# Moving the steps of seven-product groups, a weight buffer and a vector load in a two-layer fp32 decoder kernel

## The chip, the cores and the metric

The kernel runs on one core of one Trainium2 chip. A core has a matrix engine (TensorE, PE in the profile; its weight loads are PEld), a vector engine (VectorE, DVE), a scalar engine (ScalarE, ACT), a general engine (GpSimd, POOL) and a queue engine (SyncE, SP). Each works through its own instructions in order and waits for the others by semaphores; transfers between HBM and the on-chip buffers are issued here by SP and POOL. The metric is the device time of one execution in microseconds (us), the median of several runs.

## The reference

A decoder trunk of two layers over 256 tokens of width 2048, in float32. Each layer normalises its input, projects it once, sends it through three token mixers (sparse attention, a convolution module, stick-breaking attention), gates each, and merges the three by sigmoid gates before one output projection:

```python
def hybrid_layer(x, ...):
    h = rms_norm(x, norm_w)
    proj = h @ w_in
    (qa, ka, va, za, qi, ki, wi, ub, zb, qc, kc, vc, zc, gates) = jnp.split(proj, split_points(), axis=-1)
    ...
    y_a = (dsa_attention(qa, ka, va, qi, ki, wi, top_k) * jax.nn.silu(za)) @ w_a_out
    y_b = (conformer_conv(ub, conv_w, conv_b, cln_w, cln_b) * jax.nn.silu(zb)) @ w_b_out
    y_c = (stick_breaking_attention(qc, kc, vc) * jax.nn.silu(zc)) @ w_c_out
    g = jax.nn.sigmoid(gates).reshape(b, s, N_BRANCH, D_MODEL)
    merged = g[:, :, 0] * y_a + g[:, :, 1] * y_b + g[:, :, 2] * y_c
    return x + merged @ w_out

def reference(x, ...):
    for i in range(DEPTH):
        x = hybrid_layer(x, ...)
    return rms_norm(x, final_norm_w)
```

## The kernel before

**Products.** Every float32 operand is split into a high and a low part, and a product is three matmuls: high by high, low by high, high by low. The activations are split once. The weights come in units of 512 KB (128 partitions, 2 blocks of 512 columns): SP loads a unit (L413), ACT casts its high part `wh` (L247, `high`), DVE subtracts to get the low part `wl` (L251, `low`), and PE multiplies (L262). Such a unit is one step: twelve matmuls of 512 columns.

**Homes of the units.** `raw_unit` gives a unit one of five buffers called `raw` (RAWS = 5). Every sixth unit of a stage goes to the tile `va` instead, which is also the tile that holds the values of the stick-breaking attention (`va_pair`, read by PE at L1292). So there are six homes, and a load waits until its home has been read.

**Groups of seven products.** A 2 x 2 block product is done with seven half products (class `Seven`, M1 to M7; each has a half a and a half b, six matmuls each) instead of eight. Some of its weights are sums of blocks, which DVE makes: `two` loads a block into half of the tile `ar` (L469), `three` loads one into `ph` or `pl` (L478), `first_sums` adds them and the unit of M1 (L482, L483), `second_sum` (L487) and, in the output stage, `last_sum` (L491) go on in `ar`. M5, M6, M7 and M4 take their weights from these sums. Partial results are carried between the PSUM banks of a group by ACT (`copied`, L528) and DVE (`fork`, L534). The tiles `ph` and `pl` serve the stick-breaking attention too.

**Order.** A stage is a list of steps, and `run` goes through it: it loads seven steps ahead (PARTS + LOADS), converts two steps ahead (PARTS), and fires events that are tied to a step, the sums and copies among them. `gather` builds such a list from a string: `g.M1a` is half a of product M1 of the group, `y`, `c`, `d`, `e`, `f` each take the next plain step of a list of that name, `c*2` takes two. A scheduler turns the program into one instruction order for each engine; an instruction whose tile is free earlier can stand earlier in its queue than its line suggests.

**The merge and output stage of a layer** (the end of the layer's code, L1519 to L1570) runs as one list: the gates, the projection of the first and the third branch, then `zb`, sixteen plain steps that compute the gate of the second branch, and behind it the group `g1`, which computes merge gates, filled up with steps `y` that project the third branch's last columns; the group `h1`, the second branch's projection `y1`; and then the output projection. In the last layer the output has a group `o` for two of its four column chunks (`e`, `f` finish these) and plain steps for the two others: `c` (chunk 2) and `d` (chunk 3).

What the output multiplies are the merged values. A merged quarter (512 columns) is finished by DVE (L1386, L1387), transposed by DVE (L291), sent through HBM by POOL (`z`, L294) and brought back by POOL (`zy`, L300), and then split by ACT (L620) and DVE (L621) into a tile `s`; `use_m` does the last. Of a plain chunk's eight steps the first four (0 to 3) read the first two quarters, 4 and 5 the third, 6 and 7 the last. The weights of the last norm come in one 1 MB load (L1535).

## Time and profile before

| what | value |
|---|---|
| median of 3 runs (lowest, highest) | 2013.15 us (2013.05, 2013.35) |
| the profiled execution, its own time | 2015.98 us |
| its span (first to last instruction) | 2014.1 us |
| ACT, DVE busy | 1142.7 us (57%), 1715.3 us (85%) |
| mean granted clock of PE | 0.997 |
| HBM, over the span | 228 GB/s |

The table says of each engine how long it was busy in one profiled execution. A row of the timeline gives the start, the duration, the engine, the line of the code, the operation and the tiles (out<-in), and in brackets how long the engine had been idle and what it had waited for. SPq and POOLq are transfers as their engines issue them.

### The profile page before, as it was taken

What the parts mean: (1) busy time and instruction counts of PE and PEld (TensorE: products, weight loads), DVE (VectorE), ACT (ScalarE), POOL (GpSimd) and SP (SyncE); (2) the same over time, 40 slices, a digit from 0 to 9 for tenths busy, and PEclk for the clock granted to TensorE, in tenths of its full rate; (3) what the DMA queues carried; (4) which work ended last, traced back from release to release, by engine and by line L of the source; (5) the groups of instructions that cost most, each with busy time, mean ns of one, the idle gap of its engine ahead of it and who ended that gap; (6) DMA issues with size and microseconds to landing.
All of it is one profiled execution on the core that took longest, in us unless ns stands there. A gap on an engine that the chain in (4) does not pass through costs nothing.

```text
span 2014.1 us, 25976 instructions
## 1 busy us (share of the span) xinstructions
PE 1991.2 (99%) x9266; PEld 1667.6 (83%) x9266; DVE 1715.3 (85%) x2267; ACT 1142.7 (57%) x1327; POOL 171.2 (9%) x284
## 2 busy tenths in 40 slices
PE   9999999999999999999999999999999999999988
PEld 8889888888878888887888988888888788888876
DVE  8667899878989979978885779988879899798776
ACT  7555555565655556555554555455666555565544
POOL 0111112100100000011200111121001000000100
PEclk9999999999999999999999999999999999999999
DMA  7798679855767676787877886788657666767873
GB/s 272 233 285 264 187 220 294 246 178 178 212 204 245 185 221 222 236 259 250 305 229 233 282 242 191 236 275 245 178 178 218 212 218 197 244 210 237 283 239 126
DMA packets 234498, 461.70 MB, mean 229 GB/s; under 512 B 17216, under 2 KB 30016, under 8 KB 234240
## 3 DMA queue, kind: packets, MB, share of 16 engines
q1 hardware_dynamic: 214208, 399.74, 63.5%
q0 software_dynamic: 18496, 57.17, 9.2%
q10 hardware_dynamic: 1664, 3.15, 0.4%
q8 instruction: 72, 1.18, 0.2%
q14 instruction: 58, 0.48, 0.1%
HBM read 427.21 MB, written 32.77 MB: 228 GB/s over the span
## 4 chain that ended last, share of the span: by engine, by line
PE 94%; DMA 2%; DVE 2%; issue 1%; ACT 0%; POOL 0%; DVEq 0%; SPq 0%; POOLq 0%; ACTq 0%
PE acc L262 74%; PE mm L262 17%; DMA ar<-in_w_out_dram 1%; DVE wl L251 1%; DMA va<-in_w_a_dram 1%; PE mm L1099 1%; PE mm L1189 0%; DMA zy<-z 0%; DVE ar L483 0%; PE mm L1292 0%; PE mm L1157 0%; PE mm L1239 0%; ACT wh L247 0%; DMA z<-zt 0%; PE mm L866 0%
## 5 line engine op out<-in xcount | busy, mean ns | idle before, releaser
L262 PE MATMUL acc<-wh,s 128*128 128x512 f32 (+1 forms) x4528 | 1133.9, 390 | 2.5 <-ACT wh L247 2.5
L247 ACT CAST wh<-raw 128x1024 fp32r<-128x1024 f32 (+1 forms) x651 | 680.9, 1048 | 632.1 <-PE acc L262 451.8
L262 PEld LDWEIGHTS acc<-wh,s 128*128 128x128 f32 x4528 | 843.7, 188 | 169.6 <-ACT wh L247 4.5
L251 DVE TENSOR_TENSOR wl<-raw,wh 128x1024 fp32r<-128x1024 f32 (+1 forms) x652 | 789.9, 1215 | 197.4 <-ACT wh L247 195.8
L262 PE MATMUL acc<-wl,s 128*128 128x512 f32 (+1 forms) x2072 | 563.5, 389 | 3.3 <-DVE wl L251 3.1
L262 PEld LDWEIGHTS acc<-wl,s 128*128 128x128 f32 x2072 | 388.1, 188 | 83.8 <-DVE wl L251 6.0
L262 PE MATMUL mm<-wh,s 128*128 128x512 f32 x992 | 248.6, 392 | 6.7 <-ACT s L620 4.2
L294 POOL DMA_DIRECT2D z<-zt x192 | 112.1, 590 | 1404.4 <-DVE zt L291 1388.6
L262 PEld LDWEIGHTS mm<-wh,s 128*128 128x128 f32 x992 | 187.0, 189 | 47.0 <-ACT s L620 4.7
L684 DVE SCALAR_TENSOR_TENSOR s<-yT,cst,s 128x256 f32<-128x256 f32 x480 | 212.1, 479 | 0.0
L262 PE MATMUL mm<-wl,s 128*128 128x512 f32 x496 | 133.6, 392 | 0.5 <-DVE wl L251 0.5
L262 PEld LDWEIGHTS mm<-wl,s 128*128 128x128 f32 x496 | 93.6, 189 | 20.5 <-DVE wl L251 0.9
L247 ACT CAST wh<-ar 128x1024 fp32r<-128x1024 f32 x60 | 63.2, 1053 | 56.5 <-PE acc L262 21.7
L247 ACT CAST wh<-va 128x1024 fp32r<-128x1024 f32 x51 | 53.5, 1049 | 49.5 <-PE acc L262 19.7
L251 DVE TENSOR_TENSOR wl<-va,wh 128x1024 fp32r<-128x1024 f32 x51 | 62.1, 1219 | 20.4 <-ACT wh L247 20.4
L251 DVE TENSOR_TENSOR wl<-ar,wh 128x1024 fp32r<-128x1024 f32 x60 | 73.1, 1219 | 3.2 <-ACT wh L247 2.9
L262 PEld LDWEIGHTS mm<-s,wl 128*128 128x128 f32 x512 | 67.0, 191 | 5.0
L262 PE MATMUL mm<-s,wl 128*128 128x192 f32 x512 | 66.1, 271 | 0.0
L300 POOL DMA_DIRECT2D zy<-z x50 | 35.9, 719 | 298.3 <-DMA z<-zt 104.5
L291 DVE STREAM_TRANSPOSE zt<-acc 128x512 f32<-128x512 f32 (+1 forms) x68 | 45.4, 681 | 3.6 <-PE acc L262 3.0
L620 ACT CAST s<-zy 128x1024 fp32r<-128x1024 f32 x20 | 20.9, 1046 | 13.6 <-DVE zy L670 9.8
L621 DVE TENSOR_TENSOR s<-zy,s 128x1024 fp32r<-128x1024 f32 x20 | 24.4, 1221 | 3.7 <-ACT s L620 3.7
(272 smaller groups left out, 1245.7 us busy)
## 6 DMA issues: line engine op xcount, KB each, us to landing
raw<-in_w_in_dram SPq DMA_DIRECT2D x505, 512.0 KB, 4.5
raw<-in_w_out_dram SPq DMA_DIRECT2D x51, 512.0 KB, 5.4
zy<-z POOLq DMA_DIRECT2D x48, 512.0 KB, 5.8
z<-zt POOLq DMA_DIRECT2D x184, 128.0 KB, 4.4
va<-in_w_in_dram SPq DMA_DIRECT2D x30, 512.0 KB, 3.9
raw<-in_w_a_dram SPq DMA_DIRECT2D x28, 512.0 KB, 4.4
raw<-in_w_c_dram SPq DMA_DIRECT2D x28, 512.0 KB, 4.6
raw<-in_w_b_dram SPq DMA_DIRECT2D x28, 512.0 KB, 4.8
```

What stands on the lines that cost most here:

```text
L247: newest_parts[0] = nc.scalar.copy(u[1], u[0])
L251: newest_parts[1] = sub = nc.vector.tensor_sub(u[2], u[0], u[1].bitcast(F32))
L262: newest[0] = nc.tensor.matmul(o, lhsT, rhs, start=start, stop=stop, skip_group_check=True)
L291: nc.vector.transpose(tmp[:, t].rearrange("p b k i -> p k b i"), src.rearrange("p k (b c) -> p k b c", b=4, c=32))
L294: nc.gpsimd.dma_start(z[:, :, :, a, :].rearrange("t b c e -> c (t b) e"), tmp[a * 32:(a + 1) * 32].rearrange("c t b k i -> c (t b) (k i)"))
L300: nc.gpsimd.dma_start(y.rearrange("p (t a) k i -> p t (a k i)", a=4), z.rearrange("t b c a e -> (b c) t (a e)"))
L620: nc.scalar.copy(h, src)
L621: nc.vector.tensor_sub(l, src, h.bitcast(F32))
L684: nc.vector.scalar_tensor_tensor(o, yT[:, c, q:q + S], wq, o, op0=ALU.mult, op1=ALU.add)
L1099: nc.tensor.matmul(ps[:, q * S:(q + 1) * S], qi[i][:, hd, :], ki[j][:, 0, :], start=n == 0, stop=n == 2)
```

## The change

It has four parts. First, `raw_unit` gives the sixth and the twelfth unit of each stage's list a `raw` buffer; `va` is used from the eighteenth on. Second, the 1 MB load of the last norm's weights is tied to the third step of `zb`, no longer to the second step of `y1[3]`. Third, `g1` begins after fourteen of the sixteen steps of `zb`; the two others become its first steps `y`, and two `y` are taken instead of one ahead of the part called `rest`. Fourth, in the last layer's output the steps 6 and 7 of `c` stand behind M4b, and steps of `e` and `f` stand earlier.

```diff
     def raw_unit(w, k0, c0):
         ring[0] += 1
-        if ring[0] % (RAWS + 1):
+        if ring[0] % (RAWS + 1) or ring[0] < 3 * RAWS:
             raw = wp.tile([P, 2, 512], F32, tag="raw", bufs=RAWS, name=nm("raw"))
...
         if last:
-            y1[3][1].at(0, lambda: nc.sync.dma_start(fwl[0], fnw.partition_broadcast(P)))
+            zb[2].at(0, lambda: nc.sync.dma_start(fwl[0], fnw.partition_broadcast(P)))
...
-        steps += zb
-        steps += gather(begin + rest, g=g1, y=y2[2] + y2[3], c=c1, d=d1)
+        steps += zb[:14]
+        steps += gather(begin + "y*2 " + rest, g=g1, y=zb[14:] + y2[2] + y2[3], c=c1, d=d1)
...
         if last:
             steps += qs[c][:4] + gather(
-                "g.M1a d g.M5a g.M1b d g.M5b d g.M6a d g.M6b c g.M2a c g.M2b c g.M7a c g.M7b g.M3a g.M3b f g.M4a f g.M4b f*2 e*4",
+                "g.M1a d g.M5a g.M1b d g.M5b d g.M6a d g.M6b c g.M2a c g.M2b g.M7a g.M7b g.M3a e g.M3b e g.M4a f g.M4b f c*2 e*2 f*2",
                 g=o, c=qs[c][4:], d=qs[d], e=qs[p0], f=qs[p0 + 1])
```

The order of instructions moves as follows. On SP's queue, at the start of the first layer's merge stage, `va_5041` was the twelfth unit, and `ph`, `pl` and `ar` are the blocks for the first group's sums:

```order
 L413 DMA raw_5139<-in_w_in_dram 128x2x512
 L413 DMA raw_5162<-in_w_in_dram 128x2x512
-L469 DMA ar<-in_w_in_dram 128x2x512
-L413 DMA raw_5203<-in_w_in_dram 128x2x512
-L413 DMA va_5041<-in_w_a_dram 128x2x512
 L478 DMA ph_5100<-in_w_in_dram 128x2x512
 L478 DMA pl_5164<-in_w_in_dram 128x2x512
+L469 DMA ar<-in_w_in_dram 128x2x512
+L413 DMA raw_5203<-in_w_in_dram 128x2x512
 L413 DMA va_5239<-in_w_in_dram 128x2x512
 L413 DMA raw_5277<-in_w_in_dram 128x2x512
```

The twelfth unit is gone from here (it is loaded some ten places earlier, as `raw_5041`), and `ph` and `pl` stand ahead of the second half of `ar` and of the next unit. The second layer has the same.

On DVE's queue, at the start of the last layer's output stage, before the change (`s_2444` is the merged tile, `t_2901` a temporary of the merge, `wl_16252` the low part of the fourth step of `c`, `wl_16270` of M1a, `wl_16304` of M5a, `wl_16288` of the first step of `d`):

```order
L251 TENSOR_TENSOR wl_16252<-va_16107,wh_16251 128x1024
L621 TENSOR_TENSOR s_2928_16147<-s_2887_15930,s_2928_16147 128x2x256
L1386 TENSOR_TENSOR t_2901_16006<-mm_16115,t_2901_16006 128x512
L251 TENSOR_TENSOR wl_16270<-raw_16158,wh_16269 128x1024
L482 TENSOR_TENSOR pl_16199<-pl_16199,ar 128x1024
L1387 TENSOR_TENSOR s_2444_13599<-s_2444_13599,t_2901_16006 128x512
L251 TENSOR_TENSOR wl_16288<-raw_16179,wh_16287 128x1024
L291 STREAM_TRANSPOSE zt_16241<-s_2444_13599 128x4x4x32
L483 TENSOR_TENSOR ar<-ar,raw_16217 128x1024
L251 TENSOR_TENSOR wl_16304<-ar,wh_16303 128x1024
L1386 TENSOR_TENSOR t_2901_16006<-mm_16115,t_2901_16006 128x512
```

The same place after it (the names count on by one or two):

```order
L482 TENSOR_TENSOR pl_16199<-pl_16199,ar 128x1024
L251 TENSOR_TENSOR wl_16252<-va_16109,wh_16251 128x1024
L483 TENSOR_TENSOR ar<-ar,raw_16217 128x1024
L251 TENSOR_TENSOR wl_16270<-raw_16160,wh_16269 128x1024
L621 TENSOR_TENSOR s_2928_16146<-s_2888_15932,s_2928_16146 128x2x256
L621 TENSOR_TENSOR s_2929_16149<-s_2888_15932,s_2929_16149 128x2x256
L251 TENSOR_TENSOR wl_16288<-raw_16179,wh_16287 128x1024
L1386 TENSOR_TENSOR t_2902_16008<-mm_16117,t_2902_16008 128x512 x2
L1387 TENSOR_TENSOR s_2444_13599<-s_2444_13599,t_2902_16008 128x512
L251 TENSOR_TENSOR wl_16304<-ar,wh_16303 128x1024
L291 STREAM_TRANSPOSE zt_16241<-s_2444_13599 128x4x4x32
```

The sum L482 and L483 moved ahead of the conversions of `c`'s fourth step and of M1a, and the two merges L1386 stand together ahead of M5a's conversion. On PE the first step of `d` now stands ahead of M5a.

On DVE's queue further on in that stage, around the split of the last merged quarter (`s_2994`), before (`wl_16494` and `wl_16525` are the steps 6 and 7 of `c`, `wl_16515` and `wl_16543` are M7a and M7b):

```order
L251 TENSOR_TENSOR wl_16494<-raw_16417,wh_16493 128x1024
L251 TENSOR_TENSOR wl_16515<-ph_16109,wh_16514 128x1024
L251 TENSOR_TENSOR wl_16525<-va_16445,wh_16524 128x1024
L621 TENSOR_TENSOR s_2994_16488<-zy_16383,s_2994_16488 128x4x256
L251 TENSOR_TENSOR wl_16543<-pl_16199,wh_16542 128x1024
L251 TENSOR_TENSOR wl_16553<-raw_16475,wh_16552 128x1024
```

and after (`wl_16494` and `wl_16511` are M7a and M7b, `wl_16523` is M3a, `wl_16533` the first step of `e`):

```order
L251 TENSOR_TENSOR wl_16494<-ph_16111,wh_16493 128x1024
L251 TENSOR_TENSOR wl_16511<-pl_16199,wh_16510 128x1024
L251 TENSOR_TENSOR wl_16523<-raw_16443,wh_16522 128x1024
L621 TENSOR_TENSOR s_2994_16488<-zy_16383,s_2994_16488 128x4x256
L534 TENSOR_TENSOR acc_16340<-ev_16397,acc_16359 128x512
L251 TENSOR_TENSOR wl_16533<-va_16457,wh_16532 128x1024
```

The conversions of `c`'s two steps left this place; the split of the quarter keeps its own, and `fork` (L534) and the conversion of `e`'s first step now stand right behind it. ACT's queue has the same: the cast L620 of this quarter stands ahead of the cast for `e`'s first step.

The third part moves four loads (L478 and L469) and the sums of `g1` two steps ahead on SP and DVE in both layers. The load of the last norm's weights stands on SP behind the load `raw_14187`, in the first group of the last layer's merge stage, since its tile is free from there on.

## The prediction

> **What bounds the kernel now.** I read the page first, then a window late in the run for PE's undisturbed pace (its columns: length, then busy us and instructions of PE, PEld, DVE, ACT and POOL, then the granted clock, the DMA engines' share and GB/s), then PE's list of waits, then the timeline and the chain of work around the longest of them. The page, and the window:

> ```profile
> span 2014.1 us, 25976 instructions
> PE 1991.2 (99%) x9266; PEld 1667.6 (83%) x9266; DVE 1715.3 (85%) x2267; ACT 1142.7 (57%) x1327; POOL 171.2 (9%) x284
> ...
> 1964.00:1975.00 11.00, 11.00 (x50) 9.01 (x49) 9.38 (x11) 7.35 (x10) 0.00 (x0) 1.00 0.53 169
> ```

> PE (TensorE) is the bound: 99% busy, and 0.22 us for a matmul where nothing disturbs it (50 in 11.00), so 2.6 to 2.7 for a full step of twelve and 1.3 for a half step of six. The change leaves the matmuls as they are and reorders them. So only time in which PE stands still, or runs slowly, can go. Its waits (line, what it waited for, us in total, times, longest):

> ```profile
> PE mm L262 <- ACT s L620: 4.2, 1, 4.2
> PE acc L262 <- DVE wl L251: 3.1, 4, 1.8
> PE acc L262 <- ACT wh L247: 2.5, 4, 1.0
> PE mm L262 <- ACT wh L247: 2.4, 2, 1.3
> PE mm L262 <- DVE wl L251: 0.5, 1, 0.5
> ```

> These sum to 12.7 us, 0.6% of the span: the most that the change can win by waits alone. The timeline puts them at three kinds of place, which are the change's three parts: A, the start of the merge stage in each layer; B, the seven-product group behind zb; C, the last output stage.

> The profiled execution took 2015.98 us (span 2014.1 and 1.88 around it), 2.83 above the median of 2013.15. I make the sum against the profiled execution and subtract it from the median; part C says what the 2.83 may be.

> **A, the twelfth weight unit.** Times in layer 0 (start, duration, engine and line, in brackets the idle time before it):

> ```profile
> 575.20 0.37 SPq L413 DMA_DIRECT2D va<-in_w_a_dram  x1
> 575.66 0.42 SPq L478 DMA_DIRECT2D ph<-in_w_in_dram  x1
> 581.74 1.04 ACT L247 CAST wh<-va 128x1024 fp32r<-128x1024 f32 x1 [4.63 <-DMA va<-in_w_a_dram]
> 582.84 2.11 PE L262 MATMUL mm<-wh,s 128*128 128x512 f32 x8 [1.31 <-ACT wh L247]
> 583.96 1.22 DVE L482 TENSOR_TENSOR ph<-ph,ar 128x1024 f32<-128x1024 f32 x1
> 588.50 2.36 DVE L483 TENSOR_TENSOR ar<-ar,raw 128x1024 f32<-128x1024 f32 x2
> 590.93 1.45 PE L262 MATMUL acc<-wh,s 128*128 128x512 f32 x5 [1.00 <-ACT wh L247]
> 592.44 0.30 PEld L262 LDWEIGHTS acc<-wl,s 128*128 128x128 f32 x2 [0.37 <-DVE wl L251]
> 1578.57 2.14 PE L262 MATMUL mm<-wh,s 128*128 128x512 f32 x8 [1.11 <-ACT wh L247]
> 1586.66 1.45 PE L262 MATMUL acc<-wh,s 128*128 128x512 f32 x5 [0.95 <-ACT wh L247]
> ```

> The unit's home `va` is free only when the attention's last matmul has read it (575.2), so its load lands at 581.7 and PE waits 1.31. DVE, held up with it, then runs late into the sums of the first group, and PE waits 1.00 and 0.37 more. That is 2.7; with the slower matmuls right behind each wait (2.11 for eight) I put the layer's loss at 3.0, and layer 1's, with 1.11 and 0.95, at 2.6.

> After the change the unit takes a raw buffer at about 561.7, and the first wait goes. What is late next is `ph`: its tile is also free only at 575.2, and now it is the first load behind that wait, as `va` was. By va's own 6.5 us it lands at 581.7. DVE works in order and stops at L482 for it. From there nine pieces (L482, L251, L483 and L487 in turn) end with the `wl` of the first group's M1b, which PE, laid out without the old waits, needs at 590.6. Such pieces start 1.14 us apart (four between 583.96 and 588.50), so the last ends at 581.7 + 9 x 1.14 = 592.0, and PE stands 1.4 us. The gain is 3.0 - 1.4 = 1.6 in layer 0 and 2.6 - 1.4 = 1.2 in layer 1: **2.8 us**. Bounds: with `ph` landing where it lands now (575.66 + 7.4 = 583.1, row below) the wait is 2.8, and 0.2 and -0.2 are left, nothing; at 580.3 or earlier all of it goes, 5.6.

> ```profile
> DMA to landing us min/median/max: 7.4/7.4/7.4
> ```

> I take 581.7, since that is what the first load behind this very wait took.

> **B, the group starts two steps earlier.** PE's waits in the two layers, a sum that starts late in layer 0, and what that layer's two `ar` loads took:

> ```profile
> 762.69 1.23 DVE L482 TENSOR_TENSOR pl<-pl,ar 128x1024 f32<-128x1024 f32 x1 [1.45 <-DMA ar<-in_w_in_dram]
> 774.73 0.73 PE L262 MATMUL acc<-wl,s 128*128 128x512 f32 x2 [0.73 <-DVE wl L251]
> 1770.25 0.74 PE L262 MATMUL acc<-wl,s 128*128 128x512 f32 x2 [0.45 <-DVE wl L251]
> DMA to landing us min/median/max: 6.7/8.1/9.4
> ```

> The four loads and the sums move up by two full steps, 5.4 us, and two steps of zb now lie between the group's half steps: there DVE has 2.7 us of PE for a conversion, not 1.3. By a schedule laid out from these durations, the tightest `wl` is ready 0.05 us before PE needs it, and PE does not wait: gain 0.73 + 0.45 = **1.2 us**. The cover is thin. The first `ar` would be issued at 742.1 and may land at 747.8, after 5.7 us; for every us beyond that a layer waits one more. With the 6.7 us of the quicker one in the row above it lands one us late: -0.8 in both layers together, the lower bound; 1.2 is the upper. I take the upper, because these loads now leave before POOL's transfers of zb's output, with which they shared the DMA engines.

> The last norm's 1 MB weight load leaves the last output stage. By the new order it is issued behind a load of 1652.50; it finds its tile free, and the next load (about 1656.3) is first read here:

> ```profile
> 1652.50 4.17 SPq L413 DMA_DIRECT2D raw<-in_w_c_dram  x2
> 1671.36 1.05 ACT L247 CAST wh<-raw 128x1024 fp32r<-128x1024 f32 x1 [0.71 <-PE acc L262]
> ```

> There are over 10 us of cover for a transfer of 2.9 us (1 MB at 356 GB/s, next part): nothing.

> **C1, the start of the last output.** The window's columns end with the DMA engines' share and GB/s:

> ```profile
> 1905.00:1921.00 16.00, 16.00 (x72) 13.24 (x72) 13.95 (x18) 7.32 (x8) 3.06 (x5) 1.00 1.03 356
> 1905.67 0.42 SPq L1535 DMA_DIRECT2D s<-in_fnw_dram  x1
> 1907.70 12.38 DMA ar<-in_w_out_dram
> 1920.17 1.23 DVE L482 TENSOR_TENSOR pl<-pl,ar 128x1024 f32<-128x1024 f32 x1 [0.58 <-DMA ar<-in_w_out_dram]
> 1920.93 1.07 PE L262 MATMUL mm<-wl,s 128*128 128x512 f32 x4
> 1926.06 0.73 PE L262 MATMUL acc<-wl,s 128*128 128x512 f32 x2 [1.79 <-DVE wl L251]
> ```

> The queues are full, and without that 1 MB `ar` lands some 2.9 us earlier, at 1917.2. But DVE has the same pieces to do before PE gets past this place, in a new order: L482 now stands ahead of the conversion that PE needs at 1920.93, both merges (L1386) ahead of the first full step of the last chunk. Laid out piece by piece, PE's wait of 1.79 turns into one of about the same size a step earlier: **0**. Bounds: `ar` at 1915.5 lets all of 1.7 go; `ar` at 1920.08 as now costs 3 (rival 3).

> **C2, the long wait.**

> ```profile
> 1948.25 7.67 DMA zy<-z
> 1955.94 1.04 ACT L620 CAST s<-zy 128x1024 fp32r<-128x1024 f32 x1 [3.87 <-DMA zy<-z]
> 1956.89 1.04 ACT L247 CAST wh<-pl 128x1024 fp32r<-128x1024 f32 x1
> 1957.02 1.23 DVE L621 TENSOR_TENSOR s<-zy,s 128x1024 fp32r<-128x1024 f32 x1 [3.69 <-ACT s L620]
> 1957.04 2.07 PE L262 MATMUL mm<-wh,s 128*128 128x512 f32 x4 [4.24 <-ACT s L620]
> L534 DVE TENSOR_TENSOR acc<-ev,acc x20: 681/690/704, 607.1 to 1967.3; 128x512 f32<-128x512 f32 x20
> zy<-z POOLq DMA_DIRECT2D x48, 512.0 KB, 5.8
> 1957.00:1964.00 7.00, 6.96 (x18) 5.50 (x19) 2.94 (x3) 1.98 (x2) 0.00 (x0) 0.56 0.05 17
> ```

> PE reaches c's step 6 at 1952.80 (1957.04 - 4.24) and waits until the last merged quarter is back (1948.25 + 7.67 = 1955.92) and cast. The change puts two more half steps there, so PE comes to e's first step at 1952.8 + 2.6 = 1955.4. That step does not read the quarter, yet its `wh` stands behind L620 on ACT, and the L534 that it needs stands behind L621 on DVE: by the new orders both are still queued behind the same transfer. With the transfer landing at 1955.92, two matmuls start at 1955.92 + 0.02 + 1.04 + 1.04 = 1958.0, the rest when L620, L621 and L534 are through at about 1958.9. The wait is 2.6 + 0.5 = 3.1 instead of 4.24: gain **1.2 us** (rounded up). Bounds: a landing at 1957 gives 0.1; at 1954.9, a us less than the 7.67 towards the usual 5.8, it gives 2.2.

> The window behind it shows the clock at 0.56: 18 matmuls in 6.96 us, a loss of 6.96 - 18 x 0.22 = 3.0 us. It is near the 2.83 by which this execution is above the median, so I take it that the ordinary executions do not have it, and count it for nothing. [...] Whether it is there in ordinary executions, and goes, is rival 1.

> **Sum.** 2.8 + 1.2 + 0 + 1.2 = 5.2 us: 2013.15 - 5.2 = **2008.0** (2010.8 for a profiled execution that keeps the slow clock). The tail behind the last matmul keeps its instructions and is counted at nothing.

> **Rivals.**
> 1. The slow clock belongs to ordinary executions too and goes with the shorter wait: 2008.0 - 3.0 = 2005.0, and with `ph` early as well (2.8 more) 2002.2. For: 0.56 is plain in the window. Against: the 2.83.
> 2. The waits only change their names: `ph` lands as late as today (A 0), the quarter at 1957 (C2 0.1), B 1.2 holds: 2013.15 - 1.3 = 2011.9. For: the instructions that hold DVE and ACT up are still ahead in order. Here the change does not do what its order suggests.
> 3. Slower. `ar` of the last output lands late, and L482, now ahead, holds the conversion behind it. At 1920.1 it costs 3 us, and as the largest single wait becomes 3.4 in the layout, a slow clock of 3.0 more may follow; against 5.2 of gains elsewhere it decides from a landing of about 1920, and at 1924 (3.9 + 3 + 3.0 - 5.2 = 4.7) the kernel ends at 2017.9. For: this load took 12.38 us. Against: the 1 MB that made it wait is gone.

> **How the numbers follow.** Forecast 0.50 (2006 to 2010 by itself), rival 1 0.22, rival 2 0.23, rival 3 0.05. About 0.2%, 4.0 us, is what a measurement of this kernel can tell from no change, so faster means below 2009.1: 0.42 of the forecast's 0.50 and rival 1, 0.64; the rest of the forecast and rival 2, 0.31; slower 0.05. The range leaves out rival 3 and little else: 2002.0 to 2012.0.

> **What would show it.** A: no wait at the unit of 582.84, one wait of 0.5 to 1.5 us before the first group's second half, DVE idle before L482 for `ph`. B: no wait at 774 and 1770. C1: one wait of 1.5 to 3 us ahead of the last chunk's first step, `ar` at about 1917. C2: e's first step waiting 2 to 3.5 us, with the clock at 1.00 behind it. I am wrong if `ph` waits as now, if a new wait opens in B, or if the wait before e is above 4 us.

## The result, and the profile after

The changed kernel takes 2002.16 us (median of 4 runs, 2001.41 to 2004.93), the one before 2013.1 beside it (4 runs). The ratio is 0.9949, with a 95% interval of 0.9932 to 0.9966: about 10.3 us faster, 6.8 to 13.7. The time lies at the lower edge of the predicted range and 5.8 us below the predicted 2008.0. The profiled execution took 2004.93 (span 2003.1); it is 11.05 below the profiled execution before, so the two traces show the whole gain.

PE's waits after the change, from its list of waits (line, what it waited for, us in total, times, longest):

```profile
span 2003.1 us, 25982 instructions
PE acc L262 <- ACT wh L247: 2.6, 3, 2.1
PE acc L262 <- DVE wl L251: 1.3, 2, 1.2
PE mm L262 <- DVE t L1386: 1.2, 1, 1.2
PE mm L262 <- DVE wl L251: 0.6, 1, 0.6
```

12.7 us of waits have become 5.7 (both without 1.1 us at L866, which is in either trace; of both, 1.2 us lie between 930 and 1030 us, at places that the change leaves alone). That is 7.0, and the execution became 11.0 faster: some 4 us went without a wait going. To place them, I read at what time PE starts the matmul of the same number in both traces, at points where both kernels are doing the same thing:

| up to | before | after | earlier by | gained there | predicted |
|---|---|---|---|---|---|
| ahead of A, layer 0 | 576.37 | 575.74 | 0.62 | 0.6 | 0 |
| behind A, layer 0 | 597.84 | 593.96 | 3.88 | 3.3 | 1.6 |
| behind B, layer 0 | 777.58 | 772.68 | 4.90 | 1.0 | 0.7 |
| ahead of A, layer 1 | 1570.96 | 1566.37 | 4.59 | -0.3 | 0 |
| behind A, layer 1 | 1591.28 | 1585.09 | 6.20 | 1.6 | 1.2 |
| behind B, layer 1 | 1777.67 | 1770.64 | 7.03 | 0.8 | 0.5 |
| behind C1 | 1938.58 | 1930.80 | 7.78 | 0.8 | 0 |
| behind C2 | 1968.63 | 1957.61 | 11.02 | 3.2 | 1.2 |

Three places carry it: A in layer 0, A in layer 1, and C2. The rows behind them, from the timeline of the changed kernel (A of layer 1, C1, C2) and, with the landing of `ph` in layer 0 first and in layer 1 second, from the view of that tile:

```profile
DMA to landing us min/median/max: 4.7/4.7/4.7
DMA to landing us min/median/max: 6.1/6.1/6.1
1572.77 1.23 DVE L482 TENSOR_TENSOR ph<-ph,ar 128x1024 f32<-128x1024 f32 x1 [2.53 <-DMA ph<-in_w_in_dram]
1583.13 0.73 PE L262 MATMUL acc<-wl,s 128*128 128x512 f32 x2 [1.17 <-DVE wl L251]
1909.23 1.23 DVE L482 TENSOR_TENSOR pl<-pl,ar 128x1024 f32<-128x1024 f32 x1 [0.96 <-DMA ar<-in_w_out_dram]
1917.55 2.08 PE L262 MATMUL mm<-wh,s 128*128 128x512 f32 x8 [1.22 <-DVE t L1386]
1940.96 6.79 DMA zy<-z
1947.77 1.04 ACT L620 CAST s<-zy 128x1024 fp32r<-128x1024 f32 x1 [3.48 <-DMA zy<-z]
1948.72 1.04 ACT L247 CAST wh<-va 128x1024 fp32r<-128x1024 f32 x1
1949.82 3.83 PE L262 MATMUL acc<-wh,s 128*128 128x512 f32 x8 [2.08 <-ACT wh L247]
```

The waits are where the prediction put them. At the first group (A) layer 0 has none, layer 1 one of 1.17 at M1b, with DVE idle 2.53 us ahead of it because `ph` was not there. Behind zb (B) there is none. At the output's start (C1) PE now waits for the merge L1386, ahead of the first step of `d`. And e's first step (C2) waits 2.08 for a `wh` that stands behind the cast of the last quarter.

### The profile page after: what moved, and what is told of

Its sections match the earlier page's. It is cut to its first block, busy times and chain, and to the rows that moved or that the text cites. A ratio compares the mean times of both kernels' runs of the same rounds, so it can differ in the third digit from the quotient of the medians.

```text
span 2003.1 us, 25982 instructions
## 1 busy us (share of the span) xinstructions
PE 1987.1 (99%) x9266; PEld 1664.6 (83%) x9266; DVE 1715.3 (86%) x2267; ACT 1144.7 (57%) x1327; POOL 171.2 (9%) x284
## 3 DMA queue, kind: packets, MB, share of 16 engines
q8 instruction: 72, 1.18, 0.2%
## 4 chain that ended last, share of the span: by engine, by line
PE 96%; DMA 2%; DVE 1%; issue 1%; ACT 0%; POOL 0%; DVEq 0%; SPq 0%; ACTq 0%; POOLq 0%
PE acc L262 75%; PE mm L262 18%; DMA ar<-in_w_out_dram 1%; PE mm L1099 1%; DVE wl L251 1%; PE mm L1189 0%; DMA zy<-z 0%; DMA ph<-in_w_in_dram 0%; PE mm L1292 0%; PE mm L1157 0%; PE mm L1239 0%; DMA z<-zt 0%; DMA s<-in_xt_dram 0%; PE mm L1269 0%; PE mm L1160 0%
## 5 line engine op out<-in xcount | busy, mean ns | idle before, releaser
L262 PE MATMUL acc<-wh,s 128*128 128x512 f32 (+1 forms) x4528 | 1133.6, 389 | 2.7 <-ACT wh L247 2.6
L247 ACT CAST wh<-raw 128x1024 fp32r<-128x1024 f32 (+1 forms) x655 | 685.8, 1048 | 651.3 <-PE acc L262 442.6
L262 PEld LDWEIGHTS acc<-wh,s 128*128 128x128 f32 x4528 | 842.4, 188 | 170.8 <-ACT wh L247 3.9
L251 DVE TENSOR_TENSOR wl<-raw,wh 128x1024 fp32r<-128x1024 f32 (+1 forms) x656 | 796.3, 1216 | 201.4 <-ACT wh L247 199.4
L262 PE MATMUL acc<-wl,s 128*128 128x512 f32 (+1 forms) x2072 | 562.6, 388 | 1.4 <-DVE wl L251 1.3
L262 PEld LDWEIGHTS acc<-wl,s 128*128 128x128 f32 x2072 | 388.4, 188 | 81.0 <-DVE wl L251 2.7
L262 PE MATMUL mm<-wh,s 128*128 128x512 f32 x992 | 245.7, 389 | 1.2 <-DVE t L1386 1.2
L262 PEld LDWEIGHTS mm<-wh,s 128*128 128x128 f32 x992 | 185.9, 188 | 40.1 <-ACT wh L247 1.6
L262 PE MATMUL mm<-wl,s 128*128 128x512 f32 x496 | 133.0, 390 | 0.6 <-DVE wl L251 0.6
L262 PEld LDWEIGHTS mm<-wl,s 128*128 128x128 f32 x496 | 92.7, 188 | 20.8 <-DVE wl L251 1.5
L247 ACT CAST wh<-ar 128x1024 fp32r<-128x1024 f32 x60 | 63.3, 1054 | 51.0 <-PE acc L262 24.3
L251 DVE TENSOR_TENSOR wl<-ar,wh 128x1024 fp32r<-128x1024 f32 x60 | 73.3, 1221 | 6.8 <-ACT wh L247 6.8
L262 PEld LDWEIGHTS mm<-s,wl 128*128 128x128 f32 x512 | 66.9, 191 | 5.0
L247 ACT CAST wh<-va 128x1024 fp32r<-128x1024 f32 x47 | 49.3, 1049 | 38.1 <-PE mm L262 19.3
L262 PE MATMUL mm<-s,wl 128*128 128x192 f32 x512 | 66.0, 271 | 0.0
L251 DVE TENSOR_TENSOR wl<-va,wh 128x1024 fp32r<-128x1024 f32 x47 | 57.4, 1222 | 8.5 <-ACT wh L247 8.5
L621 DVE TENSOR_TENSOR s<-zy,s 128x1024 fp32r<-128x1024 f32 x20 | 24.4, 1218 | 3.3 <-ACT s L620 3.3
L620 ACT CAST s<-zy 128x1024 fp32r<-128x1024 f32 x20 | 20.9, 1047 | 9.4 <-DVE zy L670 5.9
## 6 DMA issues: line engine op xcount, KB each, us to landing
raw<-in_w_in_dram SPq DMA_DIRECT2D x505, 512.0 KB, 4.4
raw<-in_w_out_dram SPq DMA_DIRECT2D x51, 512.0 KB, 5.3
zy<-z POOLq DMA_DIRECT2D x48, 512.0 KB, 5.2
raw<-in_w_a_dram SPq DMA_DIRECT2D x30, 512.0 KB, 4.6
va<-in_w_in_dram SPq DMA_DIRECT2D x30, 512.0 KB, 4.5
raw<-in_w_c_dram SPq DMA_DIRECT2D x30, 512.0 KB, 4.8
raw<-in_w_b_dram SPq DMA_DIRECT2D x28, 512.0 KB, 4.8
```

Of the source, the lines that this page charges most:

```text
L247: newest_parts[0] = nc.scalar.copy(u[1], u[0])
L251: newest_parts[1] = sub = nc.vector.tensor_sub(u[2], u[0], u[1].bitcast(F32))
L262: newest[0] = nc.tensor.matmul(o, lhsT, rhs, start=start, stop=stop, skip_group_check=True)
L620: nc.scalar.copy(h, src)
L621: nc.vector.tensor_sub(l, src, h.bitcast(F32))
```

## The experiments

Three kinds of run: one part of the change alone; both kernels again, to see how far their waits vary from one execution to the next; and the changed kernel with one suspected cause taken away. Kernels that are compared ran on one chip, and the median that the kernel before had there is given, since it differs from chip to chip (2012.9 to 2014.6). The changes in us go by the ratio, which need not be the difference of the two medians.

**The homes of the units alone.**

```diff
-        if ring[0] % (RAWS + 1):
+        if ring[0] % (RAWS + 1) or ring[0] < 3 * RAWS:
```

> The kernel before with the homes of the sixth and twelfth unit alone changed. Theory (parts add up, each at its place): the two start-of-stage waits lose what they lost in the whole change, 3.3 us in layer 0 and 1.7 in layer 1, so 4.9 us in all, about 2008.2; the waits behind zb (0.73, 0.45), at the last output's start (1.79) and before c's step 6 (4.24) stay. ph takes between 4.7 and 6.1 us from issue. Rival (the prediction's size): ph takes 6.5 us, a wait of 1.4 stays in each layer, 2.8 us gained, 2010.3.

2008.91 us against 2014.58; ratio 0.9968 (0.9957 to 0.9980), 6.4 us. PE's waits:

```profile
PE mm L262 <- ACT s L620: 2.5, 1, 2.5
PE acc L262 <- DVE wl L251: 2.1, 3, 1.1
PE mm L866 <- DVE eps L79: 1.1, 1, 1.1
PE acc L262 <- ACT wh L247: 0.5, 2, 0.3
```

The group `mm <- ACT wh`, the wait at the twelfth unit, is gone, and none is left at the first group in either layer: `ph` landed after 4.1 and 4.9 us. The prediction's 6.5 us did not occur. The part is worth more than my 2.8 us by itself; the 1.5 us above my 4.9 lie within the interval.

**The twelfth and the sixth unit apart.** `or ring[0] == 12` and `or ring[0] == 6` in the same line, one profile each.

> The kernel before with the home of the twelfth unit alone changed. Theory (the prediction's): all of part A comes from the twelfth unit; no wait before it, and at most 1.2 us before the first group's second half. Rival: the sixth unit, which shares va with the attention's values, delays the attention; then the waits stay in part.

> The kernel before with the home of the sixth unit alone changed. Theory: nothing moves; waits of 0.3 to 1.5 us at the twelfth unit and of about 1.0 behind it stay in both layers. Rival: they go or shrink.

With the twelfth alone the waits at A are 0.19 in layer 0 and none in layer 1. With the sixth alone they all stay, as its list of waits shows (`mm <- ACT wh` twice, and the two of 1.0 us behind it among the four `acc <- ACT wh`):

```profile
PE mm L262 <- ACT s L620: 4.0, 1, 4.0
PE acc L262 <- ACT wh L247: 2.5, 4, 1.0
PE acc L262 <- DVE wl L251: 2.4, 2, 1.8
PE mm L262 <- ACT wh L247: 2.0, 2, 1.0
```

So part A is the twelfth unit's, as far as one profile of each can show.

**The earlier start of g1 alone.**

```diff
-        steps += zb
-        steps += gather(begin + rest, g=g1, y=y2[2] + y2[3], c=c1, d=d1)
+        steps += zb[:14]
+        steps += gather(begin + "y*2 " + rest, g=g1, y=zb[14:] + y2[2] + y2[3], c=c1, d=d1)
```

> The kernel before with g1's earlier start alone. Theory: no wait behind zb in either layer, 1.7 us gained, about 2011.4; all other waits as before. Rival: ar lands late beside the transfers of zb's output and a wait of about 1 us opens per layer; then nothing or a loss of 0.8 us.

2011.33 us against 2014.58; ratio 0.9980 (0.9970 to 0.9990), 4.0 us with an interval of 2 to 6. Nothing waits at 774 or 1770. The first `ar` was issued at 740.46 and landed after 5.5 us; DVE stood idle 0.57 us for it:

```profile
746.02 1.23 DVE L482 TENSOR_TENSOR ph<-ph,ar 128x1024 f32<-128x1024 f32 x1 [0.57 <-DMA ar<-in_w_in_dram]
752.98 1.21 DVE L482 TENSOR_TENSOR pl<-pl,ar 128x1024 f32<-128x1024 f32 x1
```

The second sum, which waited 1.45 us before the change, waits for nothing. From the table's rows "behind A" to its rows "behind B", this kernel gains 1.8 us in the two layers against the first profile of the kernel before, and 1.1 against a second one (below): no more can be tied to the part in the trace. The 4.0 of the times holds more, and what, these runs do not say.

**The new order of the last output's steps alone** (the string of `gather` in the last layer).

> The kernel before with the new order of the last output's steps alone; the last norm's weights are loaded where they were. Theory: DVE keeps its old order at the output's start, so the wait of 1.8 us there stays; e's first step waits for the last quarter's split behind which it is queued, 2 to 3 us in place of 4.24, and the slow clock behind it is one window of 3.4 us or none, so 1.2 to 2.2 us from the wait and up to 3 from the clock in the profiled execution. Rival: what the whole change won in the output stage came from the vector load, and the wait before e is as long as the old one, 4 us or more; then nothing.

2009.08 us against 2014.58; ratio 0.9973 (0.9962 to 0.9984), 5.4 us. At the output's start DVE keeps its old order and PE its old wait (1.37 us, for M5a's `wl`). Before e's first step:

```profile
1953.25 1.05 ACT L620 CAST s<-zy 128x1024 fp32r<-128x1024 f32 x1 [2.89 <-DMA zy<-z]
1955.30 0.73 PE L262 MATMUL acc<-wh,s 128*128 128x512 f32 x2 [1.49 <-ACT wh L247]
1956.22 1.64 PE L262 MATMUL acc<-wh,s 128*128 128x512 f32 x6 [0.18 <-DVE acc L534]
```

and no half clock behind it (this execution's mean clock is 0.999). The gain before e's first step is this string's, not the vector load's.

**The load of the last norm's weights alone.**

```diff
-            y1[3][1].at(0, lambda: nc.sync.dma_start(fwl[0], fnw.partition_broadcast(P)))
+            zb[2].at(0, lambda: nc.sync.dma_start(fwl[0], fnw.partition_broadcast(P)))
```

> The kernel before with the 1 MB load of the last norm's weights alone moved. Theory: ar lands 3 to 4 us earlier, DVE takes the new order at the output's start, the wait of 1.79 becomes one of about 1.2 before d's first step: 0.6 to 0.8 us gained; the wait of 4.24 before c's step 6 stays within 0.5 us. Rival (prediction): DVE has the same work, so nothing is gained there. Second rival: the transfer was all of the wait, which goes whole, 1.8 us.

2013.05 us against 2014.58; ratio 0.9997 (0.9987 to 1.0006): no difference that can be told. In its trace DVE has the new order, and PE's wait is the merge's and shorter than any that the old order left in seven profiles (1.1 to 2.1):

```profile
1914.81 1.23 DVE L482 TENSOR_TENSOR pl<-pl,ar 128x1024 f32<-128x1024 f32 x1 [0.88 <-DMA ar<-in_w_out_dram]
1923.13 2.08 PE L262 MATMUL mm<-wh,s 128*128 128x512 f32 x8 [0.89 <-DVE t L1386]
```

So it is this load, not the order of the steps, that moved DVE's sums and merges there. Why the scheduler places them otherwise without it, these runs do not show.

**Both kernels again.**

> The kernel before once more, for a second profile of it. Theory (the parts' prices vary from execution to execution, the places do not): the same waits at the same places, 0.3 to 1.5 us at the twelfth unit, about 1.0 behind it, 0.4 to 0.8 behind zb, 1.4 to 1.9 at the last output's start, 2.5 to 4.4 before c's step 6, and one or two windows of 3.4 us at half clock behind the last. Rival (the prediction): the slow clock was an accident of the first profiled execution and is absent here.

> The changed kernel on this chip. Theory: its parts share one baseline and add up by the waits they remove, 10 to 12 us below before (about 2003 where before has 2014.6). Rival: the parts add up by the medians of the four single runs, 5.7 + 3.3 + 5.5 + 1.5 = 16 us below before.

Before 2013.02 (7 runs), after 2001.41 (4 runs, 2000.27 to 2003.78); ratio 0.9941 (0.9926 to 0.9956), 11.9 us. The parts' medians alone add up to 16; whole and parts differ by what their intervals allow, so only the traces can split the gain. The second profile of the kernel before, list of waits:

```profile
span 2013.3 us, 25976 instructions
PE mm L262 <- ACT s L620: 3.6, 1, 3.6
PE acc L262 <- DVE wl L251: 2.8, 3, 2.1
PE acc L262 <- ACT wh L247: 2.5, 4, 1.0
PE mm L262 <- ACT wh L247: 1.9, 2, 1.1
PE mm L262 <- DVE wl L251: 1.2, 1, 1.2
```

The places of A and C are the same, with sizes that move by up to 0.6 us. B is missing in layer 0, where the first profile had 0.73, and is 0.55 in layer 1. The wait of 1.2 lies at 930 us, at a place that the change leaves alone. And it has the half clock: one window (a stretch of 3.41 us at half clock, 0.50 from 1926.91 to 1930.32) behind the wait of 2.10 at C1, one behind the wait of 3.62 at C2. The slow clock was no accident of the first profile.

**The last quarter's split issued later**, in the changed kernel, so that e's first step is no longer queued behind it.

```diff
-                turned([mg(j, t) for t in range(NT)], partial(use_m, j), LATER - 3 * (j == 3))
+                turned([mg(j, t) for t in range(NT)], partial(use_m, j), LATER - 3 * (j == 3 and not last))
```

> The changed kernel with the split of the last merged quarter (L620, L621) issued three steps later on ACT and DVE, behind the conversions of e's first step and of M3b. Theory: e's first step waited only because it stood in the queues behind that split; its wait of 2 us and more goes, no half clock follows, and nothing waits for the split, since c's step 6 comes some 15 us later: 2.5 to 4.5 us below the changed kernel. Rival: e's first step waits for its own weights or bank, and the time stays.

> The late split once more, beside the kernel with the merges first on the same chip. Theory: 2.5 to 4.5 us below the changed kernel again, about 14 below before, and no slow clock behind e's first step. Rival: its gain was the chip's.

1998.68 us (ratio to before 0.9924, 0.9908 to 0.9941) and, on another chip, 1998.89 (0.9928, 0.9911 to 0.9944), where the changed kernel had 2001.41 beside the first: 2.7 us less. It beats both kernels. All waits of the first of these profiles:

```profile
PE mm L866 <- DVE eps L79: 1.1, 1, 1.1
PE mm L262 <- DVE t L1386: 1.0, 1, 1.0
PE acc L262 <- ACT wh L247: 0.5, 2, 0.3
PE acc L262 <- DVE wl L251: 0.5, 1, 0.5
```

Nothing waits before `e` or for the split itself, in either profile. So that wait was a place in two queues, as the prediction had it. The second profile has a longer wait than the others in the new order at C1, 1.91 us for the merge, and one stretch of half clock behind it (0.50 from 1917.57 to 1920.99).

**Late split, and DVE's conversion of M1a ahead of the first sum that needs `ph`.**

```diff
             def first_sums(h):
-                with tc.high_priority():
+                with issue_after(newest_parts[1].ins) if lead == 5 and h == 0 else tc.high_priority():
...
-                st["M1", h].at(-PARTS, partial(first_sums, h), True)
+                st["M1", h].at(-PARTS + (lead == 5 and h == 0), partial(first_sums, h), True)
```

> The late split and, in both layers, DVE's conversion of M1a placed ahead of the first sum that needs ph. Theory: DVE has something to do while ph lands, so the wait at the second half of the first group goes down by one piece, 1.1 us, where there is one; 0 to 1.2 us below the late split alone. Rival: that wait has another cause and stays.

1998.9 us, no better than the late split (1998.68). The wait is absent in both layers, but `ph` landed after 4.4 and 4.6 us here, and at such times the changed kernel has none either: it tells nothing of the order.

**Late split, and the two merges L1386 ahead of the sum that waits for `ar`.**

```diff
-                    nc.vector.tensor_mul(sg[t], y[t], sg[t])
+                    with tc.high_priority(offset=URGENT) if last and b == 1 and j == 3 else nullcontext(): nc.vector.tensor_mul(sg[t], y[t], sg[t])
```

> The late split, and DVE's two merges L1386 of the last quarter placed ahead of the sum that waits for the last ar load, where DVE stood idle for 1 us. Theory: the 1.0 to 1.2 us that PE waits before d's first step is DVE's order, not its amount of work; that wait goes, 1.0 us below the late split alone, and nothing opens behind it. Rival: the pieces that move behind make M5a late instead, and the wait only changes its place.

1999.51 us, 0.6 above the late split on that chip. The wait moved:

```profile
1907.91 1.23 DVE L482 TENSOR_TENSOR pl<-pl,ar 128x1024 f32<-128x1024 f32 x1 [1.31 <-DMA ar<-in_w_out_dram]
1921.08 0.74 PE L262 MATMUL acc<-wl,s 128*128 128x512 f32 x2 [1.22 <-DVE wl L251]
```

PE starts `d` in time and then waits 1.22 us for the `wl` of M1b. The rival was right: the wait only changed its place. That DVE's amount of work is the limit whatever its order is not shown by it. DVE still stands 1.31 us idle for `ar`, since two splits (L621), which it did ahead of that sum with the late split alone, now come behind it.

## Why the prediction was right, and where it was too small

The direction, the places and the mechanisms held; two terms were too small (A and C1), and one was left out (the clock).

**A was right in mechanism, and mis-sized by one number, `ph`'s transfer.** I took 6.5 us, since that is what `va`, the first load behind the same wait, had taken in the one profile. Over eight profiles with the new home (sixteen landings) it took 4.1 to 6.1 us, 4.8 in the middle. The wait follows it as laid out: none up to 4.9 us; 0.17 to 0.23 at 5.1 (three times); 0.50 and 0.52 at 5.4 and 5.5; 1.17 at 6.1. The prediction's line (none at 5.1, 1.4 at 6.5) has that slope and is 0.1 to 0.2 too low. With the measured times 3.3 and 1.6 us were won, 4.9 instead of 2.8; in the second pair of profiles 2.5 and 3.1, thus 5.6.

That 6.5 came from a single landing is not what was wrong with it: over the six profiles with the old home (twelve landings) `va` took 5.4 to 6.7 us, 6.25 in the middle. `va` was the wrong load to take it from; the step "the first load behind that wait, as `va` was" left out what stands ahead of the two. In the old order a load of `ar` and one of `raw` are issued in the last 4.5 us ahead of it (first two rows below, then `va`); in the new order (the last three rows) they stand behind `ph` and `pl`, and only one load is issued in as long a time ahead of `ph`:

```profile
570.78 0.46 SPq L469 DMA_DIRECT2D ar<-in_w_in_dram  x1
573.68 0.37 SPq L413 DMA_DIRECT2D raw<-in_w_in_dram  x1
575.20 0.37 SPq L413 DMA_DIRECT2D va<-in_w_a_dram  x1
573.07 0.37 SPq L413 DMA_DIRECT2D raw<-in_w_in_dram  x1
574.58 0.37 SPq L478 DMA_DIRECT2D ph<-in_w_in_dram  x1
575.52 0.47 SPq L469 DMA_DIRECT2D ar<-in_w_in_dram  x1
```

From 572 to 574 us, in layer 0 and just ahead of these loads, the busy share of the DMA engines is 0.98 to 1.18 in the six profiles with the old home and 0.35 to 0.59 in the eight with the new one, 0.98 and 0.43 in the first pair (the view counts a packet whole where it starts, so the share can pass 1). That the shorter transfer comes from this is likely, but no run takes it apart.

**B was right:** the waits went, with 1.8 us gained in the first pair of profiles and 1.2 in the second, against 1.2; `ar` landed after 5.3 and 6.8 us. The moved vector load cost nothing at its new place.

**C1 was put at 0, and gave 0.8.** The wait did move to the merge ahead of `d`, but it is 0.9 to 1.2 us in five profiles and 1.9 in one, against 1.1 to 2.1 in the old order. In the second pair of profiles the place gave 2.8, where the kernel before had half clock behind it. That no order of DVE's pieces would take the wait away is not shown. Rival 3 did not occur: `ar` had landed by 1909.2, and 1909.2 + 7.0 = 1916.2 on the old time scale, a us before my 1917.2. Its further 3.0 us, a slow clock behind a wait of 3.4 us, were an estimate from the 4.24 us ahead of the window at 0.56; behind a wait of 3.40 us, in the kernel with the twelfth unit alone, the clock is 1.00 (last section).

**C2's wait was right in mechanism and 1 us too long:** 2.08, and 1.99 + 0.19 and 1.49 + 0.18 in two more profiles, instead of 3.1. The transfer took 6.79 us, not 7.67, and landed as PE came to the step (1947.75 and 1947.74), not 0.5 us later; and the wait for L534 was 0.2 us at most, not 0.5. The cause, the place behind the split in ACT's and DVE's queues, was shown by moving the split.

**The step that failed is the slow clock, "count it for nothing".** I argued that the 2.83 us by which the profiled execution was above the median was the half clock. But the changed kernel's profiled execution is 2.8 above its median too, with one window only. And of the seven profiles with the old order of the output's steps six have half-clock windows around the output stage (five have them behind the wait at C2 alone, one at C1 and C2): 2, 2, 2, 2, 1, 1 and 0 of them. With the new order alone, or the whole change, it is 1, 0 and 0. A window costs about 1.5 us, an estimate from the first profile of the kernel before, where two cost 3.0, and from the rows below (9 or 10 matmuls of 0.22 us in place of 16).

The ordinary executions say the same, since each was recorded with its mean clock. In the fourteen profiles this is 0.998 or 0.999 without such a window, 0.997 or 0.998 with one, and 0.997 with two. The kernel before has 0.996 or 0.997 in 34 of 40 executions, 0.998 in six and 0.999 in none, so by these profiles 34 of them had at least one; the new order of the output's steps alone has 0.998 or 0.999 in all of seven, and the changed kernel in all of eight. So the slow clock belongs to ordinary executions, and the profiled one, with 0.997, was no exception. On average the changed kernel's clock is 0.0014 higher; of 2010 us that is 2.8 us, an estimate of what my sum did not have (it takes the half clock behind the last matmul, which every profile has, to be alike in both kernels). In the first pair of profiles it was less: of the 3.2 us won at C2, 2.2 were the wait, and some 1 us is left for the one window fewer.

Rival 1, the clock and `ph` early, is what happened. That its 2002.2 meets the measured 2002.16 is in part luck: it had nothing for C1 and less for B, and the time is close to the edge of the range.

## What to carry to other kernels

When a step is moved away from a late transfer, look at what else is queued behind the instruction that waits for this transfer, on every engine: here the steps that took its place still stood behind its cast. When a transfer is priced by another one, compare also which loads stand ahead of each: twelve landings of the old load would have given 6.25 us, and the new one took 4.8. And ask at which landing the wait vanishes; that point was known here to 0.2 us. And an idle stretch of PE can cost clock besides its own time (here a wait of 4.24 us had half clock behind it that cost some 3 us more): look for it in every execution before it is taken for an accident of one.

## What the runs showed of the hardware

Eight of the fourteen traces have half clock ahead of the last matmul. There it comes in pieces of 3.41 us, one or two in a row, on a fixed grid: in the changed kernel's trace it begins at 1950.09 and again, behind the last matmul, at 1997.88, which is 14 pieces later. What went with it in these traces was how long PE stood idle within one piece of this grid, not how long a wait was. From the windows view, cut at the grid: the changed kernel, whose wait of 2.08 us lies in one piece; below it the kernel with the twelfth unit alone, whose wait of 3.40 us falls on two.

```profile
1946.68:1950.09 3.41, 1.33 (x6) 0.83 (x5) 1.24 (x2) 2.32 (x3) 0.00 (x0) 1.00 0.48 169
1950.09:1953.51 3.42, 3.42 (x9) 2.22 (x9) 3.42 (x4) 1.57 (x2) 0.00 (x0) 0.50 0.12 28
1953.51:1956.92 3.41, 3.41 (x16) 2.80 (x15) 2.09 (x3) 2.11 (x2) 0.00 (x0) 1.00 0.86 264
```

```profile
1945.89:1949.31 3.42, 1.84 (x9) 1.19 (x7) 1.79 (x2) 1.05 (x1) 0.00 (x0) 1.00 0.93 304
1949.31:1952.72 3.41, 1.59 (x7) 1.23 (x8) 1.61 (x2) 1.99 (x2) 0.00 (x0) 1.00 0.70 254
1952.72:1956.13 3.41, 3.41 (x17) 2.80 (x16) 1.98 (x2) 1.05 (x1) 0.00 (x0) 1.00 0.00 1
```
